# Stick-breaking attention: the sums over later source blocks move from TensorE to VectorE, and the second head's value products are issued first

## The chip, the core and the metric

The kernel runs on one core of a Trainium2 chip. The metric is the device time of one launch in microseconds (us). Before the change three runs took 2504.44, 2506.77 and 2509.23 us; the median is 2506.77 us. A profile was taken of another execution of the same program, which took 2498.9 us, 2497.1 us of it from the first to the last instruction.

## The reference, cut to what matters

The program is a chain of three transformer blocks on 512 tokens of width 1024. The change touches one layer of the second block, a stick-breaking attention with 16 heads of 64 columns. Here i is a block of 128 queries:

```python
def stick_breaking_attention(q, k, v):
    for i in range(S // BLOCK):
        z = jnp.einsum('bthd,bshd->bhts', q[:, t0:kl], k[:, :kl]) * scale
        mask = s_idx < t_idx
        log_fail = jnp.where(mask, jax.nn.log_sigmoid(-z), 0.0)
        later = lax.cumsum(log_fail, axis=3, reverse=True) - log_fail
        a = jnp.where(mask, jnp.exp(jax.nn.log_sigmoid(z) + later), 0.0)
        outs.append(jnp.einsum('bhts,bshd->bthd', a, v[:, :kl]))
```

For each query, a source position s gets the weight exp(log_sigmoid(z_s) + the sum of log_sigmoid(-z) over all sources between s and the query). With e = softplus(z) this is exp(z_s minus the sum of e over s and all later sources). So a source block needs, beside a triangular sum over itself, the full column sums of every source block above it.

## The kernel before, in words

All heavy products are float32 split in two: `hi` (rounded by ScalarE, L393) and `lo`, the rest (VectorE, L394), so that TensorE can run fp32r products of each part. Weights are split in the same way by `load` (L416 DMA, L419 on ScalarE, L420 on VectorE).

`sb_pair` (one call for two heads; 8 calls, here pair 0 to pair 7) keeps scores as [source in partitions, query in columns]. Source block sb has 512 - 128*sb query columns. Two waves make up a call: the first has source blocks 1, 2 and 3 of both heads in three tiles (tile 0: blocks 1 and 3 of head 0; tile 1: the same of head 1; tile 2: block 2 of both), the second has source block 0 in two tiles. In a wave, TensorE writes z into PSUM (L1150) and adds the mask (L1153). For each tile ScalarE takes Abs, Exp and Ln (L1157 to L1159), VectorE completes softplus into `sbe` (L1161), and the split follows (L393, L394). Then TensorE adds the sums into the same PSUM bank with a matrix of -1 (`nones`) for each source block above the target, and a triangular one (`ntri`) for the block itself (L1172 in plain float32 for block 3, L1175 and L1176 for hi and lo). ScalarE takes Exp into `sba` (L1180), and TensorE multiplies by the values (L1186). A copy (L1187) ends the call.

Projections of the next group of heads, or of the gate at the end, are placed between a wave's scores and its sums (`self.fill(2)`); below they are called the fillers. Their matmuls are L429 to L431 (128x512) and L439 to L441 (128x256). VectorE also works through a background list, the `adaw` reductions of block 3 (L1393), whose 512 KB come by DMA through the same three buffers as the raw weights. After the last call come the gates and the output projection.

The order of the instructions on each engine is fixed when the program is built: a scheduler takes them by readiness under its own costs. Each engine then works through its own list in that order.

Of the kernel before, what the change touches and what calls it, by code (L numbers as in the profile page):

```python
# [9 lines left out]
F32 = mybir.dt.float32  # L10
F32R = mybir.dt.float32r
BF = mybir.dt.bfloat16
AF = mybir.ActivationFunctionType
ALU = mybir.AluOpType
AX = mybir.AxisListType

P = 128
# [3 lines left out]
ALL = slice(0, S)  # L21
# [265 lines left out]
class Net:  # L287
# [99 lines left out]

    def split(self, src):  # L390
        nc = self.nc
        h, l = self.t(F32R, "hi"), self.t(F32R, "lo")
        nc.scalar.copy(h, src)  # L393
        nc.vector.tensor_tensor(l, src, h.bitcast(F32), ALU.subtract)  # L394
        return h, l
# [732 lines left out]
    def sb_pair(self, q, k, vt, c, out, pre):  # L1128


        nc = self.nc

        place = {(1, 0): (0, 0), (3, 0): (0, 384), (1, 1): (1, 0), (3, 1): (1, 384), (2, 0): (2, 0), (2, 1): (2, 256), (0, 0): (3, 0), (0, 1): (4, 0)}
        bank = {(1, 0): (0, 0), (3, 0): (0, 384), (1, 1): (1, 0), (3, 1): (1, 384), (2, 0): (2, 0), (2, 1): (3, 0), (0, 0): (4, 0), (0, 1): (5, 0)}

        parts = [[(0, slice(0, S))], [(1, slice(0, S))], [(2, slice(0, 256)), (3, slice(256, S))], [(4, slice(0, S))], [(5, slice(0, S))]]
        roles = ["sc", "sc", "tr", "ms", "sc", "sc"]
        sp, hi, lo, pr = ([None] * 5 for _ in range(4))
        z = [None] * 6
        reg = lambda tiles, sb, par: tiles[place[sb, par][0]][:, place[sb, par][1]:place[sb, par][1] + S - sb * P]  # L1140
        zreg = lambda sb, par: z[bank[sb, par][0]][:, bank[sb, par][1]:bank[sb, par][1] + S - sb * P]
        width = lambda sl: slice(0, sl.stop - sl.start)
        po, last = None, None
        for tiles, blocks in (((0, 1, 2), (1, 2, 3)), ((3, 4), (0,))):
            for t in tiles:
                for b, _ in parts[t]:
                    z[b] = self.psa("z", roles[b])
            for sb in blocks:
                for par, r in enumerate(ROWS):
                    nc.tensor.matmul(zreg(sb, par), k[c][r, sb * P:(sb + 1) * P], q[c][r, sb * P:], start=sb < 3, stop=False, skip_group_check=True)  # L1150
            for t in tiles:
                for sb, par in [m for m in place if place[m][0] == t]:
                    nc.tensor.matmul(zreg(sb, par)[:, 0:P], self.bf["ident"], self.bf["mask_sb"], start=False, stop=False, skip_group_check=True)  # L1153
                e = self.t(F32, "sbe")
                with self.tc.issue_after(pre.ins):
                    for b, sl in parts[t]:
                        nc.scalar.activation(e[:, sl], z[b][:, width(sl)], AF.Abs)  # L1157
                    nc.scalar.activation(e, e, AF.Exp, bias=0.0, scale=-1.0)
                    nc.scalar.activation(e, e, AF.Ln, bias=1.0, scale=1.0)  # L1159
                for b, sl in parts[t]:  # L1160
                    nc.vector.scalar_tensor_tensor(e[:, sl], z[b][:, width(sl)], 0.0, e[:, sl], ALU.max, ALU.add)  # L1161
                sp[t] = e
                hi[t], lo[t] = self.split(e)
            self.fill(2)
            for t in tiles:
                for sb, par in [m for m in place if place[m][0] == t]:
                    zr = zreg(sb, par)
                    for src in range(3, sb - 1, -1):
                        dst = zr[:, (src - sb) * P:]
                        done = src == sb  # L1170
                        if src == 3:
                            nc.tensor.matmul(dst, self.c["ntri"] if done else self.nones, reg(sp, src, par), start=False, stop=done, skip_group_check=True)  # L1172
                        else:
                            w = self.ntri_r if done else self.nones_r
                            nc.tensor.matmul(dst, w, reg(hi, src, par), start=False, stop=False, skip_group_check=True)  # L1175
                            nc.tensor.matmul(dst, w, reg(lo, src, par), start=False, stop=done, skip_group_check=True)  # L1176
                pr[t] = self.t(F32, "sba")
                with self.tc.issue_after(pre.ins):
                    for b, sl in parts[t]:
                        last = nc.scalar.activation(pr[t][:, sl], z[b][:, width(sl)], AF.Exp)  # L1180
            if po is None:
                po = self.psa("sbo", "po")
            for sb in blocks:
                for par in range(2):
                    col = (sb % 2) * 256 + (2 * c + par) * 64
                    nc.tensor.matmul(po[ROWS[par], sb * P:], vt[sb // 2][:, col:col + 64], reg(pr, sb, par), start=sb == 1, stop=sb == 0, skip_group_check=True)  # L1186
        nc.vector.tensor_copy(out, po)  # L1187
        return last
# [591 lines left out]
```

## Time and profile before

| What | us |
|---|---|
| median of three runs | 2506.77 |
| profiled execution | 2498.9 |
| its span, first to last instruction | 2497.1 |
| TensorE busy in it | 2438.4 (98%) |
| VectorE busy | 1313.5 (53%) |
| ScalarE busy | 983.0 (39%) |
| the stretch of the eight pairs, first Abs to last sum | 910.7 to 1158.1 |

A matmul's duration in the trace holds its latency; what one costs in a stream is the distance from its start to the start of the next. Such distances are used below. Busy shares are averages over the whole program, and the stretch that changes is a tenth of it.

### The profile page before, as it was taken

The numbers are of one execution on the slowest core, as the hardware profiler recorded it, in microseconds if no ns is written. First come the engines' busy times: TensorE is split into PE (matmuls) and PEld (weight loads), VectorE is DVE, ScalarE is ACT, GpSimd is POOL, SyncE is SP. The second block draws the span as 40 slices with busy tenths as digits, with TensorE's granted clock in tenths as the row PEclk, the third lists the DMA queues.
The fourth block names the chain that finished last, engine by engine and source line by source line (L and its number), as shares of the span: only waits on it lengthen the run. The fifth ranks groups of instructions, "written<-read, shape, count | busy, mean of one in ns | idle before, by whom it ended". The sixth has DMA issues, their size and how long they took to land. (4 is left out here: it accounts for less than half of the span.)

```text
span 2497.1 us, 31348 instructions
## 1 busy us (share of the span) xinstructions
PE 2438.4 (98%) x12622; PEld 1994.1 (80%) x12622; DVE 1313.5 (53%) x2220; ACT 983.0 (39%) x1575; POOL 62.7 (3%) x62
## 2 busy tenths in 40 slices
PE   8999999999999999999999999999999999999998
PEld 6877788888888787777877798888898768888887
DVE  7536556774775664446555654223365465432333
ACT  5423433442444445655324533222245344322221
POOL 0000000000000000000000000000010001000001
PEclk9999999999999999999999999999999989999999
DMA  5223225433433332222322113233213101323321
GB/s 188 93 90 101 90 97 185 135 123 114 152 119 119 126 109 77 68 81 83 113 71 85 37 66 118 93 101 101 93 54 103 61 26 60 96 93 101 100 87 49
DMA packets 71746, 240.78 MB, mean 96 GB/s; under 512 B 8232, under 2 KB 11184, under 8 KB 71600
## 3 DMA queue, kind: packets, MB, share of 16 engines
q1 hardware_dynamic: 71600, 238.78, 29.1%
q8 instruction: 99, 1.62, 0.3%
q14 instruction: 47, 0.39, 0.0%
HBM read 236.64 MB, written 2.11 MB: 96 GB/s over the span
## 5 line engine op out<-in xcount | busy, mean ns | idle before, releaser
L429 PE MATMUL pm<-hi,wh 128*128 128x512 f32 (+1 forms) x2736 | 1045.1, 383 | 11.1 <-ACT hi L393 7.3
L430 PE MATMUL pm<-lo,wh 128*128 128x512 f32 (+1 forms) x2736 | 1042.8, 381 | 0.0
L431 PE MATMUL pm<-hi,wl 128*128 128x512 f32 (+1 forms) x2736 | 1040.7, 380 | 0.0
L419 ACT CAST wh<-raw 128x1024 fp32r<-128x1024 f32 (+1 forms) x372 | 382.3, 1029 | 827.0 <-PE pm L430 581.5
L420 DVE TENSOR_TENSOR wl<-raw,wh 128x1024 fp32r<-128x1024 f32 (+1 forms) x372 | 445.0, 1196 | 448.8 <-ACT wh L419 422.2
L429 PEld LDWEIGHTS pm<-hi,wh 128*128 128x128 f32 x2736 | 517.2, 189 | 110.9 <-ACT hi L393 8.9
L430 PEld LDWEIGHTS pm<-lo,wh 128*128 128x128 f32 x2736 | 517.0, 189 | 96.5 <-issue 3.8
L431 PEld LDWEIGHTS pm<-hi,wl 128*128 128x128 f32 x2736 | 516.8, 189 | 96.1 <-issue 3.6
L439 PE MATMUL pm<-wh,hi 128*128 128x256 f32 x400 | 116.0, 290 | 4.9 <-ACT vt L816 4.9
L1393 DVE CUSTOM_DVE_ANT_0 adaw<-adaw,cb 128x1024 f32<-128x1024 f32 x72 | 87.9, 1220 | 55.7 <-DMA adaw<-in_w_ada 55.5
L441 PE MATMUL pm<-wh,lo 128*128 128x256 f32 x400 | 115.1, 288 | 0.0
L440 PE MATMUL pm<-wl,hi 128*128 128x256 f32 x400 | 114.2, 286 | 0.0
L1472 DVE TENSOR_TENSOR sg<-sg,pm 128x512 f32<-128x512 f32 x44 | 30.2, 686 | 132.8 <-PE pm L431 132.7
L572 POOL TENSOR_TENSOR rc<-ms,nhalf 128x4 f32<-128x4 f32 (+2 forms) x29 | 38.6, 1333 | 2335.2 <-DVE ms L577 1779.3
L439 PEld LDWEIGHTS pm<-wh,hi 128*128 128x128 f32 x400 | 77.8, 194 | 5.8 <-ACT vt L816 5.3
L441 PEld LDWEIGHTS pm<-wh,lo 128*128 128x128 f32 x400 | 77.8, 194 | 0.5 <-issue 0.3
L440 PEld LDWEIGHTS pm<-wl,hi 128*128 128x128 f32 x400 | 77.8, 194 | 0.5 <-issue 0.2
L481 PE MATMUL pm<-hi,wh 128*128 128x256 f32 (+1 forms) x216 | 61.5, 309 | 9.9 <-ACT hi L400 7.1
L970 DVE SCALAR_TENSOR_TENSOR uy<-ur,vec,uy 128x511 f32<-128x511 f32 x88 | 65.7, 747 | 9.0 <-ACT uy L968 8.0
L258 DVE TENSOR_TENSOR acc<-acc,sq 128x512 f32<-128x512 f32 (+1 forms) x93 | 54.6, 595 | 24.0 <-ACT sq L254 22.8
L482 PE MATMUL pm<-lo,wh 128*128 128x256 f32 (+1 forms) x216 | 66.0, 307 | 0.3 <-DVE lo L1424 0.3
L483 PE MATMUL pm<-hi,wl 128*128 128x256 f32 (+1 forms) x216 | 66.2, 308 | 0.0
(350 smaller groups left out, 2363.7 us busy)
## 6 DMA issues: line engine op xcount, KB each, us to landing
raw<-in_w_gu SPq DMA_DIRECT2D x88, 512.0 KB, 3.3
adaw<-in_w_ada SPq DMA_DIRECT2D x72, 512.0 KB, 3.3
raw<-in_w_dn SPq DMA_DIRECT2D x48, 512.0 KB, 3.3
raw<-in_w_up SPq DMA_DIRECT2D x44, 512.0 KB, 3.3
raw<-in_w_g SPq DMA_DIRECT2D x16, 512.0 KB, 3.3
raw<-in_w_l0qk SPq DMA_DIRECT2D x16, 512.0 KB, 3.4
raw<-in_w_l SPq DMA_DIRECT2D x12, 512.0 KB, 3.3
X<-in_x SPq DMA_DIRECT2D x16, 256.0 KB, 5.6
```

The source lines that it names most:

```text
L419: nc.scalar.copy(wh[:, :n], raw[:, :n])
L420: nc.vector.tensor_tensor(wl[:, :n], raw[:, :n], wh[:, :n].bitcast(F32), ALU.subtract)
L429: self.nc.tensor.matmul(out, a, xh, start=start and k == 0, stop=False)
L430: self.nc.tensor.matmul(out, a, xl, start=False, stop=False)
L431: self.pe = self.nc.tensor.matmul(out, b, xh, start=False, stop=stop and k == n - 1)
L439: self.nc.tensor.matmul(out, xh[:, sl], a, start=start and k == 0, stop=False)
L440: self.nc.tensor.matmul(out, xh[:, sl], b, start=False, stop=False)
L441: self.pe = self.nc.tensor.matmul(out, xl[:, sl], a, start=False, stop=stop and k == len(x) - 1)
L482: self.nc.tensor.matmul(o[:, sl], wh[:, k], xl[:, sl], start=False, stop=False)
L483: self.nc.tensor.matmul(o[:, sl], wl[:, k], xh[:, sl], start=False, stop=k == 7)
L970: nc.vector.scalar_tensor_tensor(y[:, sh:], raw[:, :S - sh], self.v("fconv_w", 44 * (2 - sh) + f), y[:, sh:], mult, add)
L1393: nc.vector.tensor_tensor_reduce(w, w, cb, 0.5, 0.0, ALU.mult, ALU.add, mod[:, i:i + 1])
```

## The change

VectorE now adds the softplus tiles of the source blocks above a target, so that one pair of products with `nones_r` (hi and lo) serves all of them. In the first wave, block 3 is added to block 2 in place (L1170, 128x128, once a head), the sum is split again (`u`), and that sum is added to block 1 (L1176 in the new file, 128x256, once a head). In the second wave, the running sum of the three blocks is split (128x384, once a head) after the fillers have been called. Block 3's own triangular product becomes two fp32r products of 128 columns in place of one in plain float32. The order of the heads in the value products is turned round.

```diff
-                    for src in range(3, sb - 1, -1):
-                        dst = zr[:, (src - sb) * P:]
-                        done = src == sb
-                        if src == 3:
-                            nc.tensor.matmul(dst, self.c["ntri"] if done else self.nones, reg(sp, src, par), start=False, stop=done, skip_group_check=True)
-                        else:
-                            w = self.ntri_r if done else self.nones_r
-                            nc.tensor.matmul(dst, w, reg(hi, src, par), start=False, stop=False, skip_group_check=True)
-                            nc.tensor.matmul(dst, w, reg(lo, src, par), start=False, stop=done, skip_group_check=True)
+            if 2 in tiles:
+                for par in range(2):
+                    above[2, par] = [x[par][:, 3 * P:] for x in (hi, lo)], P
+                    d2 = e[2][:, 256 * par + P:256 * par + 256]
+                    nc.vector.tensor_tensor(d2, d2, e[par][:, 3 * P:], ALU.add)
+                u = self.split(e[2])
+                for par in range(2):
+                    s2 = slice(256 * par, 256 * par + 256)
+                    above[1, par] = [x[:, s2] for x in u], P
+                    d1 = e[par][:, P:3 * P]
+                    nc.vector.tensor_tensor(d1, d1, e[2][:, s2], ALU.add)
             self.fill(2)
+            if 3 in tiles:
+                for par in range(2):
+                    above[0, par] = self.split(e[par], slice(0, 3 * P)), P
...
+                    if sb < 3:
+                        w, o = above[sb, par]
+                        for x in w:
+                            nc.tensor.matmul(zr[:, o:], self.nones_r, x, start=False, stop=False, skip_group_check=True)
+                    nc.tensor.matmul(zr, self.ntri_r, reg(hi, sb, par), start=False, stop=False, skip_group_check=True)
+                    nc.tensor.matmul(zr, self.ntri_r, reg(lo, sb, par), start=False, stop=True, skip_group_check=True)
...
-                for par in range(2):
+                for par in (1, 0):
                     col = (sb % 2) * 256 + (2 * c + par) * 64
```

On TensorE, second wave of the last pair, in the kernel before: the second score product (z_8876), the masks, and the first of 48 filler matmuls (two gate projections, pm) that stand ahead of the wave's sums.

```order
L1150 MATMUL z_8876<-sqk_8170,sqk_8206 128x512
L1153 LDWEIGHTS bf_ident_170
L1153 MATMUL z_8875<-bf_mask_sb_176,bf_ident_170 128x128
L1153 LDWEIGHTS bf_ident_170
L1153 MATMUL z_8876<-bf_mask_sb_176,bf_ident_170 128x128
L429 MATMUL pm_8905<-hi_6327,wh_8901 128x512
L430 MATMUL pm_8905<-lo_6328,wh_8901 128x512
L431 MATMUL pm_8905<-hi_6327,wl_8902 128x512
L429 MATMUL pm_8905<-hi_6374,wh_8901 128x512
```

The same place in the changed kernel, where hi_9062 and lo_9063 are the split of the running sum of head 0 and z_8969 its scores:

```order
L1199 MATMUL sbo_8962<-sba_8941,svt_8343 64x128
L1152 MATMUL z_8970<-sqk_8228,sqk_8264 128x512
L1155 LDWEIGHTS bf_ident_170
L1155 MATMUL z_8969<-bf_mask_sb_176,bf_ident_170 128x128
L1155 LDWEIGHTS bf_ident_170
L1155 MATMUL z_8970<-bf_mask_sb_176,bf_ident_170 128x128
L1187 MATMUL z_8969<-hi_9062,nones_r_195 128x384
L1187 MATMUL z_8970<-hi_9066,nones_r_195 128x384
L1187 MATMUL z_8969<-lo_9063,nones_r_195 128x384
L1188 MATMUL z_8969<-hi_8979,ntri_r_197 128x512
```

No filler is left there: all of them stand earlier in the list. The score products of the two heads have also come apart; one stands ahead of the value products, the other behind them.

On VectorE, end of the first wave of pair 3 in the kernel before: the softplus of tile 2 (sbe_7763), its lo, and behind it weights and an adaw reduction.

```order
L1161 SCALAR_TENSOR_TENSOR sbe_7763<-z_7731,sbe_7763 128x256
L1161 SCALAR_TENSOR_TENSOR sbe_7763<-z_7732,sbe_7763 128x256
L394 TENSOR_TENSOR lo_7771<-sbe_7763,hi_7770 128x512
L420 TENSOR_TENSOR wl_8281<-raw_8278,wh_8280 128x1024
L420 TENSOR_TENSOR wl_8287<-raw_8284,wh_8286 128x1024
L1393 ISA adaw_8547,mod_606<-adaw_8547,cb_598 128x1024
L1393 ISA mod_606 128x1
```

The same place in the changed kernel (ISA is the adaw reduction, lo_7813 the low part of u):

```order
L1163 SCALAR_TENSOR_TENSOR sbe_7799<-z_7767,sbe_7799 128x256
L1163 SCALAR_TENSOR_TENSOR sbe_7799<-z_7768,sbe_7799 128x256
L394 TENSOR_TENSOR lo_7807<-sbe_7799,hi_7806 128x512
L1406 ISA adaw_8627,mod_606<-adaw_8627,cb_598 128x1024
L1406 ISA mod_606 128x1
L1170 TENSOR_TENSOR sbe_7799<-sbe_7799,sbe_7777 128x128
L1170 TENSOR_TENSOR sbe_7799<-sbe_7799,sbe_7788 128x128
L1176 TENSOR_TENSOR sbe_7777<-sbe_7777,sbe_7799 128x256
L1176 TENSOR_TENSOR sbe_7788<-sbe_7788,sbe_7799 128x256
L394 TENSOR_TENSOR lo_7813<-sbe_7799,hi_7812 128x512
```

Five operations that TensorE's sums wait for now follow the lo, and the adaw reduction has come in between; before, everything behind the lo was work that no sum of the wave waits for.

## Rows read from the trace of the kernel before

**Rows 1.** Windows, pairs 0 and 7: window, its length, each engine's busy us, PEclk.

```profile
910.70:945.20 34.50, 34.25 (x180) 26.70 (x177) 18.30 (x25) 18.86 (x32) 0.00 (x0) 1.00 0.36 122
1127.80:1158.10 30.30, 30.30 (x158) 24.81 (x154) 15.70 (x23) 18.50 (x30) 0.00 (x0) 1.00 0.22 70
```

**Rows 2.** Waits of TensorE, 905 to 1175: total us, times, longest.

```profile
PE pm L429 <- ACT hi L393: 3.4, 1, 3.4
PE z L1175 <- ACT hi L393: 0.3, 1, 0.3
```

**Rows 3.** Timeline of TensorE, second wave of pair 0: start, duration, instruction.

```profile
938.71 0.40 PE L431 MATMUL pm<-hi,wl 128*128 128x512 f32 x1
938.94 0.39 PE L1172 MATMUL z<-sbe,nones 128*128 128x128 f32 x2
939.08 0.36 PE L1175 MATMUL z<-hi,nones_r 128*128 128x256 f32 x1
939.28 0.28 PE L1176 MATMUL z<-lo,nones_r 128*128 128x256 f32 x1
939.40 0.34 PE L1175 MATMUL z<-hi,nones_r 128*128 128x384 f32 x1
...
941.60 1.83 PE L1186 MATMUL sbo<-sba,svt 128*64 128x512 f32 x4
```

**Rows 4.** Timeline of TensorE, pair 1, from first wave to second.

```profile
959.84 1.52 PE L1186 MATMUL sbo<-sba,svt 128*64 128x384 f32 x12
961.29 1.13 PE L1150 MATMUL z<-sqk 64*128 64x512 f32 x4
962.35 0.28 PE L1153 MATMUL z<-bf_mask_sb,bf_ident 128*128 128x128 bf16 x2
```

**Rows 5.** Timeline of TensorE, pair 2: one head's score product by itself.

```profile
988.79 1.12 PE L1150 MATMUL z<-sqk 64*128 64x512 f32 x2
989.84 0.44 PE L1186 MATMUL sbo<-sba,svt 128*64 128x256 f32 x2
```

**Rows 6.** Timeline of TensorE in block 1: an fp32r product of 128 columns.

```profile
138.36 0.22 PE L831 MATMUL pd<-R,pick 128*128 128x128 f32 x1
138.42 0.23 PE L832 MATMUL pd<-bf_mask_t,bf_ident 128*128 128x128 bf16 x1
```

**Rows 7.** Timeline of ScalarE, pair 1: Abs of tiles 0, 1, hi, Abs.

```profile
945.18 0.60 ACT L1157 ACTIVATE sbe<-z 128x512 f32<-128x512 f32 x1 [2.88 <-PE z L1153]
948.38 0.59 ACT L1157 ACTIVATE sbe<-z 128x512 f32<-128x512 f32 x1
...
954.44 0.62 ACT L393 CAST hi<-sbe 128x512 fp32r<-128x512 f32 x1 [0.88 <-DVE sbe L1161]
...
962.62 0.60 ACT L1157 ACTIVATE sbe<-z 128x512 f32<-128x512 f32 x1 [2.28 <-PE z L1153]
```

**Rows 8.** Timeline of VectorE: an adaw of pair 0, then lo's of pair 1.

```profile
913.08 1.22 DVE L1393 CUSTOM_DVE_ANT_0 adaw<-adaw,cb 128x1024 f32<-128x1024 f32 x1 [1.12 <-DMA adaw<-in_w_ada]
...
948.51 0.69 DVE L394 TENSOR_TENSOR lo<-sbe,hi 128x512 fp32r<-128x512 f32 x1 [0.69 <-ACT hi L393]
...
955.09 0.69 DVE L394 TENSOR_TENSOR lo<-sbe,hi 128x512 fp32r<-128x512 f32 x1 [0.74 <-ACT hi L393]
```

**Rows 9.** Groups by line: count, then busy us, mean ns, idle before.

```profile
L419 ACT CAST wh<-raw 128x1024 fp32r<-128x1024 f32 (+1 forms) x372 | 382.3, 1029 | 827.0 <-PE pm L430 581.5
L420 DVE TENSOR_TENSOR wl<-raw,wh 128x1024 fp32r<-128x1024 f32 (+1 forms) x372 | 445.0, 1196 | 448.8 <-ACT wh L419 422.2
L1720 DVE CUSTOM_DVE_ANT_0 fxp<-fxs,cumb 128x128 f32<-128x128 f32 x8 | 2.0, 281 | 0.3 <-PE fxs L1714 0.3
L1720 DVE CUSTOM_DVE_ANT_0 fxp<-fxs,cumb 128x384 f32<-128x384 f32 x8 | 4.2, 549 | 0.0
L949 ACT COPY aT<-tr 128x384 f32<-128x384 f32 x20 | 9.5, 477 | 23.9 <-PE tr L947 23.9
```

**Rows 10.** Windows, behind the one long wait of rows 2: columns as rows 1.

```profile
1163.40:1166.90 3.50, 3.43 (x8) 2.24 (x8) 3.50 (x6) 2.73 (x6) 0.00 (x0) 0.51 0.00 0
```

More of the change, by code (lines that the diff above doesn't have):

```diff
@@ L386, in background, with split @@
                 self.bg.pop(0)()
-    def split(self, src):
+    def split(self, src, sl=ALL):
         nc = self.nc
-        h, l = self.t(F32R, "hi"), self.t(F32R, "lo")
+        h, l, src = self.t(F32R, "hi")[:, sl], self.t(F32R, "lo")[:, sl], src[:, sl]
         nc.scalar.copy(h, src)
@@ L1137, in sb_pair @@
         roles = ["sc", "sc", "tr", "ms", "sc", "sc"]
-        sp, hi, lo, pr = ([None] * 5 for _ in range(4))
+        hi, lo, pr, e = ([None] * 5 for _ in range(4))
         z = [None] * 6
@@ L1142, in sb_pair @@
         width = lambda sl: slice(0, sl.stop - sl.start)
+        above = {}
         po, last = None, None
@@ L1153, in sb_pair @@
                     nc.tensor.matmul(zreg(sb, par)[:, 0:P], self.bf["ident"], self.bf["mask_sb"], start=False, stop=False, skip_group_check=True)
-                e = self.t(F32, "sbe")
+                e[t] = self.t(F32, "sbe")
                 with self.tc.issue_after(pre.ins):
                     for b, sl in parts[t]:
-                        nc.scalar.activation(e[:, sl], z[b][:, width(sl)], AF.Abs)
-                    nc.scalar.activation(e, e, AF.Exp, bias=0.0, scale=-1.0)
-                    nc.scalar.activation(e, e, AF.Ln, bias=1.0, scale=1.0)
+                        nc.scalar.activation(e[t][:, sl], z[b][:, width(sl)], AF.Abs)
+                    nc.scalar.activation(e[t], e[t], AF.Exp, bias=0.0, scale=-1.0)
+                    nc.scalar.activation(e[t], e[t], AF.Ln, bias=1.0, scale=1.0)
                 for b, sl in parts[t]:
-                    nc.vector.scalar_tensor_tensor(e[:, sl], z[b][:, width(sl)], 0.0, e[:, sl], ALU.max, ALU.add)
-                sp[t] = e
-                hi[t], lo[t] = self.split(e)
+                    nc.vector.scalar_tensor_tensor(e[t][:, sl], z[b][:, width(sl)], 0.0, e[t][:, sl], ALU.max, ALU.add)
+                hi[t], lo[t] = self.split(e[t])
+            if 2 in tiles:
[9 more added lines that the diff above has]
+                    nc.vector.tensor_tensor(d1, d1, e[2][:, s2], ALU.add)
             self.fill(2)
+            if 3 in tiles:
+                for par in range(2):
+                    above[0, par] = self.split(e[par], slice(0, 3 * P)), P
             for t in tiles:
```

## The prediction

> **What bounds the kernel now.** First the windows of the eight pairs: TensorE is busy in all but 0.25 us of pair 0 and in all of pair 7, ScalarE and VectorE in little over half of each, at full granted clock [rows 1]; the six pairs between read the same. Then TensorE's waits over this stretch: one of 0.3 us inside, one of 3.4 us behind it, when the gated tiles are not yet ready for the output projection [rows 2]. So TensorE's list sets the stretch of 247.4 us from 910.7 to 1158.1. Yet one wait is hidden in a busy time: the last value products of a wave take 1.76 us for what two score products of the same columns do in 1.06 us [rows 3, 4], since the second head's Exp is late. Last the timelines of ScalarE and VectorE in pair 1 [rows 7, 8]: softplus goes tile by tile, and a tile takes 948.38 - 945.18 = 3.20 us, because ScalarE stands at its hi until VectorE has finished the tile. This chain is what TensorE would wait for if its fillers ended sooner.
>
> **What leaves TensorE.** A pair loses eight float32 products of 128 columns and four fp32r products of 256. The first cost 0.14 us and make the next start later (0.20 against 0.12 us), 0.22 in all; the second 0.12 [rows 3]. That is 8 x 0.22 + 4 x 0.12 = 2.24 us. It gains eight fp32r products of 128 columns. The stretch has none; the nearest row has the next start after 0.06 us [rows 6], and the 256-column row bounds it at 0.12 [rows 3]. I take 0.07: 0.6 us. Saved 1.6 us a pair, 13 us in all (10 to 14).
>
> **What comes back on TensorE.** The score products of the two heads stood side by side in most waves and ran in 1.06 us together [rows 4]; one alone takes 1.05 [rows 5]. In the new order one goes ahead of the value products, to fill the wait for the second head's Exp, and one behind, in all 16 changes of wave (four of them were so before). Some 12 more products alone, at up to 1.05 us, return 10 to 12 us; the hidden wait of about 0.7 us in eight changes gives some 5 back. On TensorE alone the balance is -6 us or so.
>
> **What comes onto the chain.** Take a pair with nothing else in the lists. First wave: tiles 0 and 1 take 6.4 us, tile 2 comes to its hi 9.26 us after the first Abs and to its lo at 9.91 [rows 7, 8], done at 10.6. So far as before. Now follow two adds of 128 columns (0.28 us for the nearest such pass on VectorE, rows 9; the second starts earlier, 0.4 together), the cast of u (0.62 as in rows 7), and its lo (0.69): ready at 12.4. The adds into block 1 lie beside the cast. Behind the low part of u stand ten matmuls, 1.3 us by distances between 0.07 and 0.23 us [rows 3, 6]; before, most of the sums could run ahead of the last lo. End of the sums: 13.7.
>
> Change of waves: before, 2.9 us from the end of the sums (959.75) to the next Abs (962.62) [rows 4, 7]. Now 0.3 us until the first head's Exp frees its bank, one score product 1.05 [rows 5], value products 1.45 [rows 4], the other score product 1.05, and 0.27 from mask to Abs: 4.1.
>
> Second wave: two tiles, the second lo done at 3.20 + 4.03 = 7.2; then two splits of 384 columns, which the order puts behind both tiles. ScalarE's casts (0.48 each, rows 9) lie beside the lo; VectorE's two subtractions start 0.46 to 0.5 us apart (0.55 long, rows 9) and add 1.0; the last three matmuls 0.65: 8.85. Change to the next pair 3.7 (before 3.6). Together 13.7 + 4.1 + 8.85 + 3.7 = 30.35 us a pair, so 8 x 30.35 - 3.7 = 239 us for the eight, against 247.4 now. The bare chain by itself would fit.
>
> **What stands in that chain.** The weights of the fillers are cast and split on the same two engines. In both orders 26 casts stand inside the 16 waves; before, each wave that held casts had 48 or 96 filler matmuls to cover them. Now they are uncovered. A cast where ScalarE waits for VectorE anyway (0.88 us of idle at tile 2, rows 7) costs the rest and its delay, some 0.3, elsewhere nearly its 1.03; a split costs 1.15 of its 1.20 where the next step of the chain is behind it [rows 9]. An adaw costs 1.22 and its DMA: in pair 0 it held the softplus for 1.6 us [rows 8]. Read from the order of the changed kernel, wave by wave: pair 0 4.0 and 2.7 us, pair 1 1.7 and 1.3, pair 2 1.3 and 1.9, pair 3 3.6 and 1.3 (two casts before and after tile 2's Exp, then an adaw between lo and adds), pair 4 0.3 and 1.9, pair 5 3.9 and 0.8, pair 6 1.3 and 1.3, pair 7 1.3 and 0. Sum 28 us: all hidden it is 0, all at full price with late DMA 36; I keep 28.
>
> So the stretch takes 239 + 28 = 267 us, 20 more than before. A check from the other side: TensorE must then stand idle about 25 us, and the order shows where. In pair 4's first wave ten fillers (10 x 0.23 = 2.3 us, rows 3) are left against a chain of 12.4 us, in pair 2 twenty-six, in pair 7 thirty-four, and in its second wave none: idle for some 9, 6, 5 and 7 us. Filler work is not lost, it was done earlier, in waves that are longer now.
>
> **The clock.** After the 3.4 us wait the granted clock was half (0.51) for 3.5 us, though TensorE was busy throughout [rows 2, 10]; that stretch lost 1.7 us. Three or four of the new gaps are longer, and the matmuls behind them belong to the chain. I add 1 us for what of this does not fall into waits, and bound it by 0 and 6.
>
> The Trainium skill, "TensorE: Matmul & The Clock Gate" (HAM oscillation), says that a wait between bursts throttles the array again each time, and counts it as a cost of its own. By that rule each of the four gaps would cost 1.7 us, 7 in all, and the sum would be 27 instead of 21; the one gap here [rows 2, 10] agrees with it, but whether it falls on the chain four times no row shows.
>
> **Elsewhere.** Inputs and output of the stretch stay. The tail (last Exp, value products, copy, gating) begins later and is as long as before. The gates are ready sooner, but the first gated tile waits for the last pair's Exp. The value products' new order alone gives nothing: both heads' products then wait for the second Exp, with a score product in the gap, as counted.
>
> **Sum.** 20 + 1 = 21 us on the profiled execution's own 2498.9 gives 2520. The median of the runs is 7.9 us above that execution, so 2528 is the time for it.
>
> **Rivals.** (a) *TensorE stays the bound.* Its list loses matmul work, and before there was no idle [rows 1, 2]; if casts and adaw hid fully and the order's fillers reached, the stretch would go with TensorE's balance and be bounded by the bare chain: -6 to -8 us, 2500. For it: the bare chain of 239 us lies below 247.4. Against it: ten and zero fillers where the chain is 12 and 8 us long. It decides if the uncovered casts cost under about 6 us together. 8%. (b) *Half of the casts hide*, mostly in ScalarE's stalls of rows 7: stretch 239 + 14, +6 us, 2513 with no clock loss. 17%, of which 7% falls within 5 us. (c) *The gaps cost more*: the half clock on each (7 us) and adaw waits like that of rows 8 in pairs 3 and 5 (another 5 to 8 us): 2541. 15%. The forecast has 60%, from 2518 to 2537.
>
> What a measurement can tell from no change is about 0.2%, 5 us. Faster by more than that: case (a), 8%; within: 7%; slower: 85%. The range reaches from (b) to (c): 2511 to 2541.
>
> **What would show it.** Right: TensorE's waits between 905 and 1190 grow from 0.3 to 20 us or more, released by the lo and hi splits of `sbe`; the longest in pairs 2, 4 and 7, several us each; the granted clock falls to half behind them; about 268 us from the first Abs to the last sum; score products alone between value products. Wrong: TensorE idle under 5 us there and the last sum before 1160; or fp32r products of 128 columns at 0.2 us each, which would slow it for another reason. It would also be wrong if ScalarE's casts lay in its stalls almost everywhere.

## The result and the profile after

The changed kernel takes 2541.76 us, the median of four runs, against 2505.61 for the kernel before in the same session: 1.0148 times as long, 95% interval 1.0116 to 1.0181. A second session gave 1.0156 (1.0139 to 1.0174). It is slower by some 36 us; the forecast was 21 us, and the range to 2541 ended just below. The profiled execution has a span of 2536.1 us against 2497.1.

Of these 39.0 us 37.6 lie in the eight pairs: from the first Abs to the start of the last sum they take 284.8 us (910.2 to 1195.0) instead of 247.2. First TensorE's waits from 905 to 1215, which answer to [rows 2].

```profile
PE z L1187 <- DVE sbe L1163: 14.2, 3, 7.1
PE z L1187 <- ACT hi L393: 8.1, 4, 6.9
PE pm L429 <- ACT hi L393: 3.3, 1, 3.3
```

The third row is the old wait ahead of the output projection. The first two are new: 22 us where 0.3 stood. They are three waits ahead of first waves (3.8, 7.1, 3.4 us in pairs 2, 4, 7), one of 6.9 in pair 7's second wave, and three of 0.4. Now the windows of pairs 0, 2, 4 and 7 (as in [rows 1], the clock third from the right).

```profile
910.19:947.62 37.43, 36.89 (x186) 27.68 (x184) 20.84 (x32) 20.36 (x36) 0.00 (x0) 1.00 0.35 113
980.88:1018.48 37.60, 33.45 (x150) 23.26 (x149) 16.33 (x26) 19.21 (x34) 0.00 (x0) 0.82 0.13 42
1054.48:1090.97 36.49, 29.05 (x134) 19.94 (x133) 16.29 (x27) 18.44 (x32) 0.00 (x0) 0.81 0.13 44
1161.45:1195.00 33.55, 22.64 (x82) 15.42 (x80) 14.39 (x24) 17.75 (x31) 0.00 (x0) 0.73 0.15 47
```

Pair 0 has no long wait and full clock; the other three have a mean clock of 0.73 to 0.82. What that means for the chain is to be seen in pair 2, in TensorE's timeline behind the wait.

```profile
986.54 0.39 PE L431 MATMUL pm<-hi,wl 128*128 128x512 f32 x1
990.69 0.47 PE L1187 MATMUL z<-hi,nones_r 128*128 128x128 f32 x1 [3.77 <-DVE sbe L1163]
...
995.07 0.52 PE L1189 MATMUL z<-lo,ntri_r 128*128 128x384 f32 x1
995.39 0.31 PE L1188 MATMUL z<-hi,ntri_r 128*128 128x128 f32 x1
...
997.12 2.07 PE L1152 MATMUL z<-sqk 64*128 64x512 f32 x2
999.12 2.40 PE L1199 MATMUL sbo<-sba,svt 128*64 128x384 f32 x8
1000.45 1.49 PE L1199 MATMUL sbo<-sba,svt 128*64 128x256 f32 x8
1001.88 1.57 PE L1152 MATMUL z<-sqk 64*128 64x512 f32 x2
1003.38 0.28 PE L1155 MATMUL z<-bf_mask_sb,bf_ident 128*128 128x128 bf16 x2
```

A product of 384 columns costs 0.32 us from start to start (0.17 to 0.18 in the kernel before), one head's score product 2.00 (1.05 in [rows 5]). Windows of 2 us over the same place:

```profile
988.00:990.00 2.00, 0.00 (x0) 0.00 (x0) 1.64 (x2) 1.94 (x5) 0.00 (x0) 0.79 0.00 0
994.00:996.00 2.00, 2.00 (x8) 1.77 (x8) 1.51 (x3) 0.06 (x1) 0.00 (x0) 0.50 0.00 0
998.00:1000.00 2.00, 2.00 (x6) 0.48 (x6) 0.00 (x0) 0.37 (x2) 0.00 (x0) 0.50 0.00 0
1002.00:1004.00 2.00, 2.00 (x6) 0.94 (x7) 0.00 (x0) 0.36 (x1) 0.00 (x0) 0.80 0.00 0
```

The clock falls to half (1.2 GHz) inside the wait at 989.2 and comes back at 1002.8, though TensorE is busy without a break from 994 on: 13.7 us, against 3.5 in [rows 10]. The others lasted 13.7 (pair 4), 10.2 and 20.5 us (pair 7 and what follows), 45.4 us of the stretch in all.

The next table is worked out from the trace's matmuls. Each is charged with the time to the next one's start, less idle, in us, from the first Abs to the last sum; the same 767 records of filler products lie in this stretch in every kernel shown. The kernel keep_busy2 comes from the experiments.

| | before | after | keep_busy2 |
|---|---|---|---|
| fillers | 145.8 | 147.7 | 147.9 |
| score products | 24.6 | 38.6 | 35.3 |
| value products | 26.2 | 22.2 | 18.6 |
| sums | 46.7 | 48.6 | 38.0 |
| zero products | | | 26.8 |
| idle | 0.3 | 23.9 | 3.0 |
| stretch (with masks) | 247.2 | 284.8 | 273.2 |
| of it at half clock | 0 | 45.4 | 0 |

### The profile page after: what moved, and what is told of

Read it like the earlier page. It is cut to its first block, busy times and chain, and to the rows that moved or that the text cites. A ratio compares the mean times of both kernels' runs of the same rounds, so it can differ in the third digit from the quotient of the medians.

```text
span 2536.1 us, 31251 instructions
## 1 busy us (share of the span) xinstructions
PE 2452.5 (97%) x12526; PEld 1994.2 (79%) x12526; DVE 1335.7 (53%) x2276; ACT 994.8 (39%) x1599; POOL 62.7 (2%) x62
## 5 line engine op out<-in xcount | busy, mean ns | idle before, releaser
L572 POOL TENSOR_TENSOR rc<-ms,nhalf 128x4 f32<-128x4 f32 (+2 forms) x29 | 38.6, 1333 | 2375.5 <-DVE ms L577 1820.6
L1163 DVE SCALAR_TENSOR_TENSOR sbe<-z,sbe 128x512 f32<-128x512 f32 (+1 forms) x48 | 28.2, 601 | 79.7 <-ACT sbe L1161 79.7
```

## The experiments

Ratios are to the kernel before in the same session, with 95% intervals; "pairs" is the stretch in the profiled execution, followed by TensorE's idle time and the time at half clock in it. The expectations stand as they were written; each edit is against the changed kernel unless it says otherwise.

| kernel | median us | ratio | pairs, idle, half clock |
|---|---|---|---|
| keep_busy | 2543.6 | 1.0167 (1.0146 to 1.0188) | 287.3, 11.8, 23.9 |
| values_back | 2540.2 | 1.0154 (1.0131 to 1.0178) | 284.4, 24.0, 34.7 |
| wave1_only | 2509.9 | 1.0033 (1.0017 to 1.0049) | 255.2, 2.4, 0 |
| wave2_only | 2518.2 | 1.0065 (1.0044 to 1.0087) | 265.3, 11.4, 18.4 |
| keep_busy2 | 2530.3 | 1.0112 (1.0094 to 1.0130) | 273.2, 3.0, 0 |
| wave1_back | 2514.7 | 1.0048 (1.0030 to 1.0066) | 258.7, 2.3, 0 |
| one_weight | 2527.6 | 1.0105 (1.0085 to 1.0125) | 258.2, 5.5, 13.7 |
| best | 2512.7 | 1.0038 (1.0026 to 1.0051) | 252.7, 6.2, 3.4 |
| values_only | 2501.3 | 0.9999 (0.9984 to 1.0014) | 246.5, 0.3, 0 |
| early | 2526.1 | 1.0092 (1.0068 to 1.0115) | 273.4, 14.1, 27.5 |
| changed_again | 2541.2 | 1.0156 (1.0139 to 1.0174) | 288.9, 23.5, 55.9 |
| early_busy | 2518.5 | 1.0062 (1.0046 to 1.0079) | 264.0, 2.7, 0 |

### TensorE kept busy in its waits

```diff
+IDLE = {(2, 0): 17, (4, 0): 30, (7, 0): 14, (7, 3): 30}
...
+    def keep(self, z, x, n):
+        with self.tc.issue_after(self.pe.ins): [self.nc.tensor.matmul(z, self.zero_r, x, start=False, stop=False, skip_group_check=True) for _ in range(n)]
...
-            self.fill(2)
+            self.fill(2); self.keep(z[parts[tiles[0]][0][0]], hi[tiles[0]], IDLE.get((self.pair, tiles[0]), 0))
```

> The changed kernel, with 17, 30, 14 and 30 fp32r products of 512 columns and zero weights put on TensorE in the first waves of pairs 2, 4 and 7 and the second wave of pair 7, where it waited 3.8, 7.1, 3.4 and 6.9 us; they add zero to a bank of scores. Theory (the clock term was sized too small): per pair the walk of the prediction fits pairs 0, 1, 3, 5 and 6 within 1.5 us and misses pairs 2, 4 and 7 by 4, 4 and 8 us, just those with half clock behind a wait. So with TensorE busy the granted clock stays 1.00 from 905 to 1200 and about 16 us go: 2526 us (2520 to 2531). Rival (the chain of casts, splits and adds was priced too low there, the half clock lies beside it): nothing goes, 2538 or more, even at full clock.

Measured 2543.6 us: nothing gained, and the test had failed to set its condition, since the clock did not stay full. Its timeline in pair 2:

```profile
994.42 0.51 PE L1188 MATMUL z<-hi,ntri_r 128*128 128x256 f32 x2 [1.03 <-ACT hi L393]
995.77 0.50 PE L1189 MATMUL z<-lo,ntri_r 128*128 128x256 f32 x2 [0.84 <-DVE lo L394]
996.95 0.51 PE L1187 MATMUL z<-hi,nones_r 128*128 128x256 f32 x2 [0.68 <-ACT hi L393]
```

The zero products ended too early, the sums then waited in three pieces, and half clock followed at 998.2. In pair 7's second wave the zero products themselves waited 3.3 us. Of these three pairs only pair 4 kept the full clock, and it took 33.3 us instead of 36.5. So it was done again with more of them.

```diff
+IDLE = {(2, 0): 25, (4, 0): 34, (7, 0): 22, (7, 3): 32}
...
+            self.fill(2); self.keep(z[0 if tiles[0] == 0 else 2], hi[0], IDLE.get((self.pair, tiles[0]), 0))
```

> As keep_busy, since there the second waits and the wait ahead of the zero products still brought half clock in pairs 2 and 7 while pair 4, at full clock, went from 36.5 to 33.3 us: 25, 34 and 22 zero products in the first waves of pairs 2, 4 and 7, and 32 in pair 7's second wave, there into a bank that is free from its start. Clock theory: no half clock from 905 to 1195, pairs 2 and 4 take 33.5 us each (37.6 and 36.5 in the changed kernel), pair 7 four to eight us less, so 2527 us (2521 to 2533). Rival (what the pairs gain is lost by the zero products standing ahead of the sums): 2538 or more, at full clock.

Measured 2530.3 us. The windows of its pairs 0, 2, 4 and 7:

```profile
910.87:948.37 37.50, 36.94 (x186) 27.61 (x183) 20.92 (x32) 20.34 (x35) 0.00 (x0) 1.00 0.34 113
981.50:1015.10 33.60, 33.57 (x175) 24.38 (x174) 16.40 (x26) 19.29 (x33) 0.00 (x0) 1.00 0.14 48
1051.10:1084.60 33.50, 32.08 (x168) 23.42 (x167) 16.29 (x27) 18.47 (x32) 0.00 (x0) 1.00 0.14 47
1155.40:1184.10 28.70, 28.70 (x137) 21.78 (x134) 14.55 (x24) 17.45 (x31) 0.00 (x0) 1.00 0.17 55
```

Pair 0, left alone, is as long as in the changed kernel. Pairs 2, 4 and 7 are 4.0, 3.0 and 4.9 us shorter at full clock, though TensorE was given 113 products more. The pairs take 11.6 us less. The clock theory's range (2521 to 2533) held. Of the 16 us that it began with 2.4 were never there: by the prediction's own terms pair 7 misses by 5.6 us (33.5 against 30.35 - 3.7 + 1.3), not by 8.

Zero products could also have gained by shifting other work. In pair 4 no instruction of ScalarE or VectorE stands in another place, and on TensorE only two sums do. The low part of u, the split of the added tile, starts there 12.4 us after the first Abs in the changed kernel and 12.5 in keep_busy2; the difference lies behind it, up to the next Abs. The lo and the Abs, first in the changed kernel, then in keep_busy2:

```profile
1066.88 0.69 DVE L394 TENSOR_TENSOR lo<-sbe,hi 128x512 fp32r<-128x512 f32 x1
1076.17 0.60 ACT L1159 ACTIVATE sbe<-z 128x512 f32<-128x512 f32 x1 [4.53 <-PE z L1155]
```

```profile
1063.79 0.69 DVE L394 TENSOR_TENSOR lo<-sbe,hi 128x512 fp32r<-128x512 f32 x1
1069.95 0.60 ACT L1159 ACTIVATE sbe<-z 128x512 f32<-128x512 f32 x1 [2.64 <-PE z L1155]
```

That is 9.3 us against 6.2. The same step loses 3.8 us in pair 2 and 3.3 in pair 7, and pair 7's last sums lose 0.9: 11.2 of the 11.6 us lie where sums, score and value products run at half clock. In pairs 2 and 7 one weight cast and its split do stand elsewhere; that is worth 0.1 us in pair 2, and in pair 7 1.6 us in the first wave, of which 0.9 come back in the second.

### The same change twice, and the clock's price once more

> The changed kernel once more, beside early_busy in one session. All theories: 1.4 to 1.6 % over the kernel before, half clock behind the waits of pairs 2, 4 and 7, some 40 us of it among the eight pairs.

Nothing is edited here. Measured 2541.2 us, with 55.9 us at half clock in the pairs where some 40 were expected. The windows of pairs 2 and 4:

```profile
981.03:1020.46 39.43, 35.28 (x150) 24.27 (x149) 16.32 (x26) 19.22 (x33) 0.00 (x0) 0.78 0.12 41
1056.44:1095.53 39.09, 31.71 (x134) 21.30 (x133) 16.28 (x27) 18.44 (x33) 0.00 (x0) 0.74 0.12 41
```

The instructions and TensorE's waits are those of the first profile (14.2 and 8.1 us). The half clock lasted 17.1 and 20.5 us instead of 13.7 twice, and these two pairs took 1.8 and 2.6 us more; the other six agree within 0.3. One program, two lengths of half clock, and the time goes with it.

The zero products were put into early as well, a kernel that is told below:

```diff
+IDLE = {(2, 0): 18, (4, 0): 22, (7, 0): 6, (7, 3): 18}
```

> Kernel early with 18, 22 and 6 zero products in the first waves of pairs 2, 4 and 7 and 18 in pair 7's second wave, as in keep_busy2. Early has 14 us of waits and 27 us of half clock in the eight pairs. Clock theory, with the price measured in keep_busy2 (11.6 us for 45 us of half clock): 7 us go, the eight pairs take 266 us instead of 273, the whole 2519 us (2514 to 2524). Rival (in keep_busy2 it was not the clock, but the other order of fillers, that gained): 2526 or more, at full clock.

Measured 2518.5 us, the pairs 264.0 instead of 273.4. Pairs 2 and 4 of early, then of early_busy:

```profile
978.45:1016.52 38.07, 34.47 (x145) 23.05 (x144) 16.92 (x28) 19.11 (x34) 0.00 (x0) 0.87 0.17 56
1048.46:1088.21 39.75, 35.15 (x143) 22.66 (x143) 18.01 (x29) 19.28 (x33) 0.00 (x0) 0.83 0.18 63
```

```profile
980.23:1013.67 33.44, 33.44 (x162) 23.30 (x161) 16.98 (x28) 19.23 (x34) 0.00 (x0) 1.00 0.19 63
1045.71:1079.90 34.19, 34.16 (x167) 23.69 (x167) 18.18 (x29) 19.19 (x34) 0.00 (x0) 1.00 0.22 74
```

A second kernel gains where its clock stays full: 9.4 us with 27.5 less at half clock, 11.6 with 45.4 less in keep_busy2. This one is less clean: casts and splits moved as well, and u's low part is done 1.4 and 2.8 us earlier in pairs 2 and 4, counted from the first Abs of each. From there to the next Abs they gain 4.2 and 3.6 us.

### One half of the change at a time

```diff
-                    d1 = e[par][:, P:3 * P]
-                    nc.vector.tensor_tensor(d1, d1, e[2][:, s2], ALU.add)
...
-                    above[0, par] = self.split(e[par], slice(0, 3 * P)), P
...
+                        w = [(above[sb, par][1], x) for x in above[sb, par][0]] if sb else [((s - sb) * P, reg(x, s, par)) for s in (3, 2, 1) for x in (hi, lo)]
```

> The changed kernel with block 0 (the second wave) summed source by source again, each by its hi and lo part; the adds into block 1 and the splits of 384 columns are gone, the sums of the first wave stay on VectorE. Chain theory: 1.0 to 1.15 us a pair go from the second wave, 9 us, and the wait in pair 7's second wave gets shorter, so about 2530 us (2524 to 2535). Rival (the second wave holds most of the cost): 2515 or less. Second rival (the splits of 384 columns lie in waits anyway): 2538 or more.

```diff
-                u = self.split(e[2])
...
+                        w = [((s - sb) * P, reg(x, s, par)) for s in range(3, sb, -1) for x in (hi, lo)] if sb else [(P, x) for x in above[sb, par][0]]
```

> The changed kernel with blocks 1 and 2 (the first wave) summed source by source again, each by its hi and lo part; the split u of the added tile is gone, the adds stay for the second wave. Chain theory: the first wave's walk falls from 13.7 to about 11.3 us, 19 us in all, the waits in the first waves of pairs 2, 4 and 7 shrink by some 2 us each and with them the stretches at half clock, so 2518 us (2510 to 2524). Rival (the casts between the tiles set the waits whatever the sums are): 2535 or more.

Measured: 2509.9 with the first wave's part alone, 2518.2 with the second wave's. The second is what the chain theory said. The first misses its 2530 by far and falls to the rival that the second wave holds most of the cost. Inside its pairs TensorE hardly waits (its longest answers for 905 to 1167):

```profile
PE z L1188 <- ACT hi L393: 0.7, 2, 0.5
PE z L1152 <- ACT sba L1193: 0.5, 2, 0.3
```

So the longer first-wave chain is covered while the second wave leaves fillers over (the second waves use 193 of the 767, the first waves of pairs 2 and 4 have 56 each; in the changed kernel 300, 26 and 10), and no half clock comes. Against the kernel before, the pairs lose 8.0 us by the first part, 18.1 by the second (18.4 us at half clock) and 37.6 by both (45.4). The parts do not add up. Both draw on the same fillers, and with both the clock falls behind the last filler: at full clock (keep_busy2) the loss would be 26.0. That these two things are the whole of it is not shown.

### The order of the value products

```diff
-                for par in (1, 0):
+                for par in range(2):
```

> The changed kernel with the first head's value products first again. Chain theory: both orders take the same time from the last sum to the next Abs (two Exp of 0.6 us and value products of 1.45 against a score product of 1.05 and the same value products), so 2541 us, between 2535 and 2547, though TensorE's list gets some 10 us shorter by score products that stand in pairs again. Rival (the torn pairs of score products are what costs): 2530 or less.

Measured 2540.2, as the chain theory had it. The reverse edit on the kernel before:

> The kernel before with only the second head's value products first. TensorE is its bound, so its list decides: torn pairs of score products add some 10 to 12 us (measured +10.7 in keep_busy2), the waits hidden in the value products go, some 7 us (measured 7.6 there): +3 to +5 us, 2506 us (2500 to 2512). Rival (the order is what makes the changed kernel slow): 2520 or more.

Measured 2501.3, no difference (0.9984 to 1.0014), a little below what I expected: torn score products cost 6.6 us there and the waits hidden in the value products gave 7.6 back. And back again on wave1_only, which has no long waits:

> The changed kernel with block 0 summed source by source (as wave1_only, which had no wait of TensorE inside the eight pairs and took 8 us more than the kernel before) and the first head's value products first again. Theory (where TensorE is the bound, torn pairs of score products cost what the prediction said, 10 us): 2500 us, at or below the kernel before. Rival (wave1_only is slow by the walk of the first wave, hidden behind fillers): 2508 or more.

Measured 2514.7, slower than wave1_only by its pairs (258.7 against 255.2): the score products cost 6.7 us less, the value products, which hold a wait again, 10.3 more. The theory that torn score products are the cost falls: in this kernel the head order is worth nothing or a few us in favour of the change. How they are torn, in wave1_only:

```profile
962.39 1.12 PE L1152 MATMUL z<-sqk 64*128 64x512 f32 x2
963.44 1.52 PE L1199 MATMUL sbo<-sba,svt 128*64 128x384 f32 x12
964.89 1.12 PE L1152 MATMUL z<-sqk 64*128 64x512 f32 x2
```

2.10 us for the two score products, against 1.06 side by side in [rows 4].

### Weight casts out of the chain

```diff
+        if kept and self.kept:
+            return [x.rearrange("p (k g) -> p k g", g=g) for x in self.kept]
...
```

Inside the pairs `load` hands out its first tiles again. The loads, casts and splits of the others are left out, so the kernel computes something else and is of use for its times alone.

> The changed kernel, in which the projections inside the eight pairs all use the first of their weight tiles: their loads, casts and splits (some 26 of each) are left out, the products stay; five instead of six buffers for weights everywhere. Chain theory: of the 28 us that casts, splits and adaw add to the chain, all but the adaw's 6 to 8 go, so the stretch takes about 247 us, the waits of pairs 2 and 4 nearly vanish and with them the half clock: 2510 us (2500 to 2518). Rival (the casts lie in stalls, the sums alone make the waits): 2530 or more.

Measured 2527.6 for the whole, which is neither theory's number. But the whole is no measure here: outside the pairs this execution took 15 us more than the changed kernel's (2524.6 - 258.2 against 2536.1 - 284.8), with one weight buffer of six less and 87.0 us there at half clock against 64.5; which of the two costs what is not shown. The pairs fell from 284.8 to 258.2. All adaw work in the stretch was also drawn into pair 0. Pairs 1 and 3, which are the bare chain:

```profile
953.02:984.23 31.21, 30.80 (x194) 24.16 (x193) 10.48 (x19) 18.04 (x34) 0.00 (x0) 1.00 0.00 1
1016.27:1047.16 30.89, 30.68 (x183) 23.23 (x182) 10.48 (x19) 18.04 (x35) 0.00 (x0) 1.00 0.00 1
```

Pairs 1, 3, 5 and 6 take 124.4 us together. In keep_busy2, with casts and adaw, they take 140.0: 15.6 us more, where the prediction's wave-by-wave prices for these pairs sum to 15.2. Of the others pair 0, with the adaw, took 36.6 us, and pair 4 37.7, with four waits of 0.2 to 0.7 and then half clock for 13.7. These two are why the pairs did not fall to the expected 247.

### Splits of the second wave earlier, and the best that came of it

```diff
                     nc.vector.tensor_tensor(d1, d1, e[2][:, s2], ALU.add)
+                    above[0, par] = self.split(e[par], slice(0, 3 * P)), P
             self.fill(2)
-            if 3 in tiles:
-                for par in range(2):
-                    above[0, par] = self.split(e[par], slice(0, 3 * P)), P
```

> The changed kernel with the splits of the added blocks for the second wave issued right behind the adds of the first, ahead of its Exp, and not behind the second wave's tiles. Chain theory: the second waves get 1.0 us shorter (two subtractions at 0.5 us), the first ones stay, since ScalarE and VectorE wait there for TensorE's sums: 8 us less chain, pair 7's last wait falls from 6.9 to 6 us, so the eight pairs take 277 us instead of 285 and the whole 2533 us (2526 to 2538). Rival (the splits then delay the split u or the Exp of the first wave by as much): 2539 or more.

Measured 2526.1, twice the expected gain. The pairs fell by 11.4 us where 8 were expected, and the half clock in them from 45.4 to 27.5. ScalarE in the changed kernel, second wave of pair 1, then early in the same wave:

```profile
967.20 0.60 ACT L1159 ACTIVATE sbe<-z 128x512 f32<-128x512 f32 x1 [2.64 <-PE z L1155]
...
973.89 1.45 ACT L393 CAST hi<-sbe 128x512 fp32r<-128x512 f32 x3 [0.76 <-DVE sbe L1163]
976.70 0.60 ACT L1193 ACTIVATE sba<-z 128x512 f32<-128x512 f32 x1 [1.36 <-PE z L1189]
977.53 0.60 ACT L1193 ACTIVATE sba<-z 128x512 f32<-128x512 f32 x1 [0.23 <-PE z L1189]
```

```profile
966.02 0.60 ACT L1159 ACTIVATE sbe<-z 128x512 f32<-128x512 f32 x1 [3.93 <-PE z L1155]
...
973.03 0.59 ACT L1193 ACTIVATE sba<-z 128x512 f32<-128x512 f32 x1
975.10 0.60 ACT L1193 ACTIVATE sba<-z 128x512 f32<-128x512 f32 x1 [1.48 <-PE z L1189]
```

Behind both tiles three casts stand in a row, tile 4's and the two of the added blocks (x3). With the two moved to the first wave, the first head's Exp starts 7.0 us after the first Abs instead of 9.5, and the last one 9.1 instead of 10.3. The term of 1.0 us was right for this wave (1.2). But the first wave of pair 1 took 1.0 us longer (20.6 against 19.6 from Abs to Abs), so the pair as a whole gained 0.2: there the rival, that the splits delay the first wave, holds. Over the eight pairs the second waves took 18.0 us less and the first ones 6.5 more. At full clock (early_busy against keep_busy2) the pairs take 264.0 instead of 273.2 us, 9.2 less; the other 2.2 of the 11.4 is what half clock cost less. In the other waves the fillers came to stand otherwise; I did not take those apart.

```diff
-                u = self.split(e[2])
...
+                    above[0, par] = self.split(e[par], slice(0, 3 * P)), P
...
-                    above[0, par] = self.split(e[par], slice(0, 3 * P)), P
...
+                        w = [((s - sb) * P, reg(x, s, par)) for s in range(3, sb, -1) for x in (hi, lo)] if sb else [(P, x) for x in above[sb, par][0]]
...
-                for par in (1, 0):
+                for par in range(2):
```

> What the experiments point to: no split u and no sums by VectorE in the first wave (each source by its hi and lo part in fp32r, block 3 too), the added blocks are split for the second wave right behind the first wave's tiles, ahead of its Exp, where ScalarE waits for TensorE; the first head's values first. TensorE loses some 1.4 us a pair against the kernel before (six float32 products to two fp32r ones, six products less in the second wave), no step of the chain gets longer: 2497 us (2490 to 2503). Rival (ScalarE and VectorE have no room ahead of the second wave, the splits delay its scores): 2505 or more.

Measured 2512.7 where 2497 was expected: not better than the kernel before, and the rival's number. Sums cost TensorE 43.5 us instead of 46.7, but it waited 6.2 us, the longest 2.4. No version here beats the kernel before. The pairs hold 5.5 of the 9 to 10 us. The profiled execution, the slowest of twelve, is 18.1 us longer than that of the kernel before; 12.6 of it lie outside the pairs, with 86.7 us at half clock there against 60.5. What brings the clock down in those places I did not find.

## Why the prediction was wrong

The direction, the place and the cause of the waits came as forecast; the step that failed is **the clock**: "I add 1 us for what of this does not fall into waits, and bound it by 0 and 6". It cost some 11 us. The profile's own numbers close the sum: the forecast chain of 267 us, 6 us of chain that it missed, and 11.6 us between half and full clock, 11.2 of them traced to it, make the 284.8.

- **TensorE idle about 25 us, longest in pairs 2, 4 and 7.** Right: 23.9 us; 4, 7, 3 and 7 us where 6, 9, 5 and 7 were foretold.
- **The bare chain of 30.35 us a pair.** Right within 3%: one_weight ran 30.9 to 31.2, so some 0.75 a pair or 6 us in all were missing. At full clock its first wave was right step by step: in one_weight the low part of u is done after 12.5 us (12.4 foretold), and from its end the next Abs comes 5.5 us later in most pairs (5.4 foretold: 1.3 and 4.1). At half clock that last step took 8.6 to 9.3 us in pairs 2, 4 and 7 of the changed kernel, and 9.9 in pair 4 of one_weight: this is where the clock fell on the chain. The change to the next pair took 4.7 from the last lo, not 4.35.
- **Casts, splits and adaw, 28 us.** Right where it could be tested: 15.6 measured, 15.2 foretold in four pairs. At full clock the pairs take 273.2 us, that is 267 and the missing 6.
- **TensorE's savings of 13 us.** Too high: the sums fell by 8.7 (46.7 to 38.0). Torn score products returned 10.7, within the 10 to 12; the hidden waits gave 7.6 back, not 5. An fp32r product of 128 columns, taken at 0.07, cost up to 0.11 (last section). It mattered little, since waits set the time.
- **The clock, 1 us.** Wrong. I took the loss from one place, 1.7 us behind a wait [rows 10], where a dense stream of the output projection's products followed and half clock ended after 3.5 us, and let most of it fall into waits. In the changed kernel the sums, score and value products follow, all on the chain, and half clock lasted 10 to 20 us; what ends it no run here shows. TensorE's products lost 17.5 us (after against keep_busy2: scores 3.3, values 3.6, sums 10.6); keep_busy2's zero products and idle are 29.8 us where the changed kernel waits 23.9, so 5.9 of it falls into waits that full clock would have had, and 11.6 remain. The Trainium skill, "TensorE: Matmul & The Clock Gate" (HAM oscillation), from which the prediction drew 7 us, counts the loss as half of the time at half clock; that would be 22.7 us of the 45.4. Its direction was right against mine. Its figure holds for the time in which TensorE worked: about 10 of the 45.4 us are waits (1.5, 3.2 and 5.0 behind the fall in pairs 2 and 4 and pair 7's second wave), and half of the other 35 is the 17.5 that the products lost. The stretch as a whole lost less.
- **The values' order alone gives nothing.** Right (values_only, values_back).
- **The tail is as long as before.** Nearly: last sum to copy 3.4 us instead of 2.2, at half clock; behind it 0.7 us more up to the last instruction.
- **Rivals.** The cause that (c) named, half clock on each gap, is the one that came, but that its time of 2541 is nearly the one measured is luck: it was put together from 7 us of clock and 5 to 8 of adaw waits. The clock cost 11, the bare chain 6 more than foretold, and the adaw waits did not come onto the chain: in the eight pairs VectorE waits 11.6 us for adaw's transfers, 8.2 before, and the ones in pairs 3 and 5 (3.4 and 3.3 us) lie behind the first wave's splits and end just ahead of the second wave. That it had 15% was an error of the price, not of the mechanism.

## What to carry to other kernels

Where fillers cover a dependent chain, count how many are left at each wave: lengthening one wave only moves them, and the wave that runs out waits. Price such a wait by what TensorE does behind it, not by its own length: if the chain's own products follow, they all run at half clock until it returns. Two changes that each cost little (8 and 18 us) can cost more together (38, of which 26 at full clock) once their waits bring the clock down.

## What the runs showed of the hardware

- Half clock behind a wait had no fixed length: for the same program, waits and place it lasted 13.7 us in one execution and 20.5 in another, with TensorE busy for most of it.
- One long wait is not needed: in keep_busy three waits of 1.0, 0.8 and 0.7 us within 5 us came before the fall, in one_weight four of 0.2 to 0.7.
- Products with zero weights, which change no result, held the clock at 1.00 where there were enough of them, and the pairs were 11.6 and 9.4 us shorter. In keep_busy, with 91 of them against keep_busy2's 113, the clock still fell in two of three pairs, and the whole gained nothing.
- An fp32r product of 128 columns cost mostly 0.06 or 0.11 us from start to start at full clock. With the triangular matrix it was 0.06 where the next product has the same weights, and at least 0.11 where it has others; with the matrix of -1 both values occur ahead of the same weights. In wave1_only:

```profile
960.03 0.22 PE L1187 MATMUL z<-hi,nones_r 128*128 128x128 f32 x1
960.09 0.28 PE L1187 MATMUL z<-lo,nones_r 128*128 128x128 f32 x1
960.20 0.33 PE L1188 MATMUL z<-hi,ntri_r 128*128 128x256 f32 x1
```

The prediction took 0.07 for each; the pair of hi and lo here gives 0.085, a part of the savings that did not come.
